# One encoder layer on one core: the first FFN product starts on six tiles' unmixed blocks, and no tile pair is computed plainly

## The chip, the cores and the metric

The kernel runs on one core of a Trainium2 chip. TensorE (PE in the profile) multiplies matrices, VectorE (DVE), ScalarE (ACT) and GpSimd (POOL) work on tiles in SBUF, and DMA queues, issued here by SyncE (SP), move tiles between HBM and SBUF. The metric is the device time of one execution in microseconds (us); lower is better.

## The reference

The layer is a hybrid attention block and then a gated feed-forward network (FFN), over 1024 tokens of 1024 channels, in float32. Only the second part is touched by the change:

```
h2 = rms_norm(x, g_norm2) * (1.0 + sc2) + sh2     # 1024 x 1024
a, up = split(h2 @ w_ffn_in, 2)                   # 1024 x 2816 each
x = x + gt2 * ((silu(a) * up) @ w_ffn_out)
```

The first product, `h2 @ w_ffn_in`, is called FFN1 below.

## The kernel before

**Three passes.** Every float32 operand of a large product is split in two parts, `hi` and `lo`, both in fp32r, and each 128 x 128 x 512 step is three matmuls (hi·hi, hi·lo, lo·hi: `PASS`). A weight block is loaded with `wload` (256 KB, a `raw` tile, 6 buffers) and split with `wsplit`: ACT copies it to `hi` (L101), POOL or, where the caller names it, DVE subtracts to get `lo` (L102). There are 10 `hi` and 10 `lo` buffers, used in turn; a split therefore can't be written before PE has read the split that stood ten places earlier.

**FFN1 in tiles.** The 2816 channels of `a` and `up` are 22 tiles of 128; tile `j` and tile `j + 11` (`HT` is 11) go together in the second FFN product. For one tile the product is a 2 x 2 block product: rows are a and up, the inner blocks are the two halves of the 1024 channels, the columns are the two halves of the tokens. `blk(k, c)` is channel half `k` of token half `c` in `h2T`. A plain tile needs 8 block products of 4 k-steps times 3 passes, 96 matmuls. A tile in the seven-product (Winograd) form needs 7, 84 matmuls: four of them use the mixed token blocks `t1` to `t4`, sums and differences of the four `blk`, and three use unmixed blocks (`w11` with `blk(0,0)`, `w12` with `blk(1,0)`, `x4` with `blk(1,1)`). The weights `x1` to `x4` are sums and differences too, made by `pair_weights` on DVE (L1068, L1069) and POOL (L1076, L1080). `make_t` builds the mixed blocks row by row: for each of 4 rows, 4 additions of hi and lo (L1040, half on POOL), 4 differences (L1042 to L1045), 4 ACT copies (L1048) and 4 subtractions (L1049).

**The order.** PE's order is the program's. The other engines' orders are laid out by a planner at build time, by readiness and then by program order. Ahead of FFN1 stands the output projection in three sweeps of token rows; after each sweep `o_post` finishes the residual and the norm of its token tiles (last step on POOL, L936), and `o_turn` transposes them on PE (L945) into `h2T` (L949, L950). Tokens 0 to 767 are in `h2T` when FFN1 begins; those of tiles 6 and 7 are still in `o_post`. So FFN1 runs tiles 0 and 11 plainly: first their token half 0, 96 matmuls, then `o_turn(6)` and `o_turn(7)`, then `pair_weights` of tile 1 and `make_t` (in program order), then the other token half, 96 matmuls, and from there the pairs (1, 12), (2, 13) and so on by `ffn1_pair`. Tile 1 (`first`) has its three unmixed products first.

**After the products.** `silu_up` applies the sigmoid (ACT, L994), multiplies (DVE L995, POOL L996) and stores; when the second tile of a pair is done it also makes four combinations for the second FFN product (L1003 to L1006). These tiles, the outputs `c11` to `c22`, and the temporaries of `make_t` share one tag `c` with `NC` = 11 buffers. `bank` gives PSUM banks: 4 tags (t, v, d, s) with 2 buffers each.

Of the kernel before, what the change touches and what calls it, by code (L numbers as in the profile page):

```python
# [10 lines left out]
F32 = mybir.dt.float32  # L11
F32R = mybir.dt.float32r
AF = mybir.ActivationFunctionType
# [7 lines left out]
HT = 11  # L21
EPS = 1e-6
NEG = -1e30
NRAW, NHL = 6, 10
NC = 11
W2C = ((), (0,), (1, 2), (3,), (4, 5), (6, 7), (8, 9), (10,))
PP, QT, AQ, AT, AV = 100, 0, 0, 0, 0
WARM = 40
# [7 lines left out]
def hybrid_layer(ctx: ExitStack, tc: tile.TileContext, x, colp, wada1, wada2, bada2, wqkv, wg, wpa, wpb,  # L36
                 wo, w1, w2, hgain, ropeg, rope, rbias, bmask, g2r, out):
    nc = tc.nc

    def pool(name, side, **kw):  # L40
        return tc.alloc_tile_pool(name=name, bufs=1, side=side, reuse_waits="tile", **kw)

    const = pool("const", "left")
    wp = pool("w", "left")
# [13 lines left out]
    def bank(tag):  # L58
        return ps.tile([128, 512], F32, tag=tag, name="ps_" + tag)
# [32 lines left out]
    def wload(src, n):  # L92
        raw = wp.tile([128, 512], F32, tag="raw", bufs=NRAW, name="raw")
        nc.sync.dma_start(raw[:, :n], src)
        return raw[:, :n]

    def wsplit(r, eng=None):
        n = r.shape[1]
        hi = wp.tile([128, 512], F32R, tag="hi", bufs=NHL, name="whi")
        lo = wp.tile([128, 512], F32R, tag="lo", bufs=NHL, name="wlo")  # L100
        nc.scalar.activation(hi[:, :n], r, AF.Copy)  # L101
        (eng or nc.gpsimd).tensor_sub(lo[:, :n], r, fview(hi[:, :n]))  # L102
        return hi, lo

    def wslot(src, n):
        return wsplit(wload(src, n))
# [13 lines left out]
    PASS = ((0, 0), (0, 1), (1, 0))  # L120
# [448 lines left out]
    def mm_set(pb, wsl, src, ksrc, n, ntot, done, hs):  # L569
        for j in range(n):  # L570
            for i, (a, b) in enumerate(PASS):
                nc.tensor.matmul(pb, wsl[a][:, j * 128:(j + 1) * 128], src[b][:, ksrc + j, hs],  # L572
                                 start=(done == 0 and j == 0 and i == 0),
                                 stop=(done + j == ntot - 1 and i == 2))
# [161 lines left out]
    for n in range(6, 92):  # L736
        u, t = divmod(n, 8)
# [70 lines left out]
    mgp = pool("merged", "right")  # L808
# [97 lines left out]
    h2T = [h2p.tile([128, KT, S], F32R, name=f"h2T{i}") for i in range(2)]  # L906
# [77 lines left out]
            for t in ts:  # L984
                o_post(t, [pb[t, 0], pb[t, 1]])

    glate = []
    wj = {}

    gt = {}  # L990
# [1 line left out]
    def silu_up(j, hf, a, up):  # L992
        sg = gt[j, hf] = half_tile("c", NC)
        nc.scalar.activation(sg, a, AF.Sigmoid)  # L994
        nc.vector.tensor_mul(sg, sg, a)  # L995
        nc.gpsimd.tensor_mul(sg, sg, up) if j not in (0, HT) else nc.vector.tensor_mul(sg, sg, up)  # L996
        r, k = divmod(j, HT)
        n = {(0, 0): 0, (1, 0): 1, (1, 1): 2}.get((r, hf))
        if n is not None:
            nc.sync.dma_start(ga_d[n, k], sg)  # L1000
        if r == 1 and hf == 1:
            a11, a21, a12, a22 = (gt[z] for z in ((k, 0), (k, 1), (j, 0), (j, 1)))
            nc.gpsimd.tensor_add(a22, a21, a22)  # L1003
            nc.gpsimd.tensor_sub(a21, a11, a21)
            nc.gpsimd.tensor_sub(a11, a22, a11)
            nc.vector.tensor_sub(a12, a12, a11)  # L1006
            for n, z in enumerate((a22, a11, a21, a12)):
                nc.sync.dma_start(ga_d[3 + n, k], z)

    def ffn1(j, hf):  # L1010
        if j not in wj:
            wj[j] = [wslot(w1[j, :, 4 * q:4 * q + 4, :], 512) for q in range(4)]
        w = wj[j]
        hs = slice(hf * 512, hf * 512 + 512)
        tg = {(0, 0): "vv", (HT, 1): "tt"}.get((j, hf), "ds")
        pa, pu = bank(tg[0]), bank(tg[1])
        for q in range(2):
            mm_set(pa, w[q], h2T, 4 * q, 4, 8, 4 * q, hs)
        for q in range(2):
            mm_set(pu, w[2 + q], h2T, 4 * q, 4, 8, 4 * q, hs)  # L1020

        def post():
            silu_up(j, hf, pa, pu)

        glate.append(post) if glate is not None else post()

    def blk(k, c):
        return [z[:, 4 * k:4 * k + 4, 512 * c:512 * c + 512] for z in h2T]

    def half_tile(tag, bufs):  # L1030
        return sp.tile([128, 512], F32, tag=tag, bufs=bufs, name=tag)

    def make_t():
        tb = [[sp.tile([128, 4, 512], F32R, name=f"t{n}{i}") for i in range(2)] for n in range(4)]
        b = {(k, c): blk(k, c) for k in range(2) for c in range(2)}
        for k in range(4):
            y = {}
            for n, kc in enumerate(((0, 1), (0, 0), (1, 1), (1, 0))):
                y[kc] = half_tile("c", NC)
                (nc.gpsimd if n % 2 else nc.vector).tensor_add(y[kc], fview(b[kc][0][:, k]), fview(b[kc][1][:, k]))  # L1040
            y11, y12, y21, y22 = y[0, 0], y[0, 1], y[1, 0], y[1, 1]
            nc.vector.tensor_sub(y11, y12, y11)  # L1042
            nc.vector.tensor_sub(y12, y22, y12)
            nc.vector.tensor_sub(y22, y22, y11)
            nc.gpsimd.tensor_sub(y21, y21, y22)  # L1045
            for n, z in enumerate((y11, y22, y12, y21)):
                hi, lo = tb[n][0][:, k], tb[n][1][:, k]
                nc.scalar.activation(hi, z, AF.Copy)  # L1048
                (nc.gpsimd if n == 3 else nc.vector).tensor_sub(lo, z, fview(hi))  # L1049
        return tb  # L1050

    nprod = [0]

    def prod(w, b):
        nprod[0] += 1
        pb = bank("tvds"[nprod[0] % 4])
        for k in range(4):
            for i, (p, q) in enumerate(PASS):
                nc.tensor.matmul(pb, w[p][:, k * 128:(k + 1) * 128], b[q][:, k],  # L1059
                                 start=(k == 0 and i == 0), stop=(k == 3 and i == 2))  # L1060
        return pb

    def pair_weights(j, part):
        if part == 0:
            r = wj[j] = {q: wload(w1[j, :, 4 * q:4 * q + 4, :], 512) for q in (0, 2, 3, 1)}
            r["w11"] = wsplit(r[0])
            s1, s2 = (wp.tile([128, 512], F32, tag="raw", bufs=NRAW, name="ws") for _ in range(2))
            nc.vector.tensor_add(s1, r[2], r[3])  # L1068
            nc.vector.tensor_sub(s2, s1, r[0])  # L1069
            r["x2"] = wsplit(s2, nc.vector)  # L1070
            r["w12"] = wsplit(r[1])
            r["s1"], r["s2"] = s1, s2
            return
        r = wj[j]
        s3, s4 = r[2], r["s2"]
        nc.gpsimd.tensor_sub(s3, r[0], s3)  # L1076
        r["x3"] = wsplit(s3, nc.vector)
        r["x1"] = wsplit(r["s1"])
        r["w22"] = wsplit(r[3])
        nc.gpsimd.tensor_sub(s4, r[1], s4)  # L1080
        r["x4"] = wsplit(s4, nc.vector)

    def ffn1_pair(j, first=False):
        for part in range(2):
            if not first:
                pair_weights(j, part)
        w11, x2, w12, x3, x1, w22, x4 = (wj[j][z] for z in ("w11", "x2", "w12", "x3", "x1", "w22", "x4"))
        t1, t2, t3, t4 = tb
        p1 = prod(w11, blk(0, 0))
        c11 = half_tile("c", NC)  # L1090
        nc.scalar.activation(c11, p1, AF.Copy)
        if first:
            p2 = prod(w12, blk(1, 0))
            p3 = prod(x4, blk(1, 1))
        p6 = prod(x2, t2)
        c12 = half_tile("c", NC)
        nc.vector.tensor_add(c12, c11, p6)
        if not first:
            p2 = prod(w12, blk(1, 0))
        nc.vector.tensor_add(c11, c11, p2)  # L1100
        p7 = prod(x3, t3)
        c21 = half_tile("c", NC)
        c22 = half_tile("c", NC)
        nc.vector.tensor_add(c21, c12, p7)
        p5 = prod(x1, t1)
        nc.vector.tensor_add(c22, c21, p5)
        nc.vector.tensor_add(c12, c12, p5)
        p4 = prod(w22, t4)
        nc.vector.tensor_add(c21, c21, p4)  # L1109
        silu_up(j, 0, c11, c21)  # L1110
        if not first:
            p3 = prod(x4, blk(1, 1))
        nc.vector.tensor_add(c12, c12, p3)
        silu_up(j, 1, c12, c22)

    first = 1
    for j, hf in ((0, 0), (HT, 0), (0, 1), (HT, 1)):
        ffn1(j, hf)
        if (j, hf) == (HT, 0):
            o_turn(6)  # L1120
            o_turn(7)
            wop.release()
            mgp.release()
            sp = pool("st", "right")
            for f in glate:
                f()
            glate = None
            pair_weights(first, 0)
            pair_weights(first, 1)
            tb = make_t()  # L1130
    for k in range(1, HT):
        ffn1_pair(k, k == 1)
        ffn1_pair(k + HT)
    sp.release()
    h2p.release()

# [182 lines left out]
```

## Time and profile before

| | |
|---|---|
| Median of 3 runs | 1606.36 us (1603.22 to 1607.03) |
| The profiled execution: its own time | 1605.34 us |
| Its span, first to last instruction | 1603.6 us |
| PE busy | 1542.5 us of the span |
| DVE, ACT, POOL busy | 1026.6, 667.1, 717.3 us |

The span is what the views of the trace cover; 1.7 us lie around it. Time 0 of a view is the start of the span. A line such as L1059 is a line of the kernel before; L1059 is the matmul of `prod`, L572 that of the plain tiles (`mm_set`). Busy time of a matmul includes the time in which it overlaps the next one.

### The profile page before, as it was taken

The page shows a single profiled execution, that of the slowest core. Times are in us where ns is not written, and L with a number is a line of the kernel's source. Part 1 is how long each engine was busy: PE and PEld are TensorE (multiplying, and loading weights), DVE is VectorE, ACT ScalarE, POOL GpSimd, SP SyncE. Part 2 cuts the span into 40 slices and gives each one's busy share as a digit, 9 for nine tenths or more (in the row PEclk, how much of TensorE's full clock was granted, in tenths as well). Part 3 has the DMA queues.
Part 4 walks back from the last instruction along what each step waited for, and adds up shares of the span by engine and source line. Part 5 has one row for each costly group of instructions (what it writes and reads, how often), then busy time and mean ns, then how long its engine had stood idle before and what let it go on. Part 6 is the DMA issues. An engine that isn't in the chain of part 4 may idle for free.

```text
span 1603.6 us, 24772 instructions
## 1 busy us (share of the span) xinstructions
PE 1542.5 (96%) x8240; PEld 1289.0 (80%) x8240; DVE 1026.6 (64%) x2188; ACT 667.1 (42%) x1734; POOL 717.3 (45%) x672
## 2 busy tenths in 40 slices
PE   8999999999999999999999886999999999999997
PEld 7888888898888777778887675788888888888886
DVE  6766676766988743342438869866666666435466
ACT  5555555555645443412234533323333333344442
POOL 1432232221101041554425576876666666545566
PEclk9999999999999999999999998999999999999999
DMA  9322231344244351776645531333333333576765
GB/s 342 101 99 80 84 114 46 125 126 128 88 129 134 92 170 61 264 233 208 210 161 175 177 93 40 104 114 105 101 107 101 106 99 119 191 217 197 243 217 177
DMA packets 149056, 227.52 MB, mean 142 GB/s; under 512 B 27312, under 2 KB 65072, under 8 KB 148928
## 3 DMA queue, kind: packets, MB, share of 16 engines
q1 hardware_dynamic: 148928, 225.94, 44.1%
q8 instruction: 65, 1.06, 0.3%
q14 instruction: 63, 0.52, 0.1%
HBM read 172.28 MB, written 53.59 MB: 141 GB/s over the span
## 4 chain that ended last, share of the span: by engine, by line
PE 75%; DVE 12%; DMA 6%; issue 3%; ACT 2%; POOL 2%; SPq 0%; POOLq 0%; DVEq 0%; ACTq 0%
PE ps_d L283 14%; PE ps_t L1059 6%; PE ps_s L1059 6%; PE ps_v L1059 6%; PE ps_d L1059 6%; PE ps_d L594 4%; PE ps_s L572 3%; PE ps_d L572 3%; PE ps_s L1161 3%; PE ps_d L1161 3%; PE ps_v L475 2%; PE ps_s L434 2%; PE ps_v L1161 2%; PE ps_t L1161 2%; PE ps_t L572 2%
## 5 line engine op out<-in xcount | busy, mean ns | idle before, releaser
L102 POOL TENSOR_TENSOR wlo<-raw,whi 128x512 fp32r<-128x512 f32 (+2 forms) x269 | 362.2, 1354 | 466.6 <-ACT whi L101 442.7
L101 ACT ACTIVATE whi<-raw 128x512 fp32r<-128x512 f32 (+2 forms) x418 | 244.1, 604 | 435.3 <-DMA raw<-in_wg_dram 70.9
L283 PE MATMUL ps_d<-whi,hT 128*128 128x384 f32 x1152 | 316.9, 343 | 0.5 <-ACT v L318 0.5
L102 DVE TENSOR_TENSOR wlo<-raw,whi 128x512 fp32r<-128x512 f32 (+1 forms) x149 | 150.9, 1022 | 130.3 <-ACT whi L101 119.9
L283 PEld LDWEIGHTS ps_d<-whi,hT 128*128 128x128 f32 x1152 | 210.3, 188 | 6.2 <-ACT vs L321 3.5
L283 PE MATMUL ps_d<-wlo,hT 128*128 128x384 f32 x576 | 193.7, 336 | 0.9 <-POOL wlo L102 0.9
L283 PEld LDWEIGHTS ps_d<-wlo,hT 128*128 128x128 f32 x576 | 108.5, 188 | 1.5 <-POOL wlo L102 1.5
L313 POOL TENSOR_TENSOR ra<-qn,rtab 128x64 f32<-128x64 f32 x48 | 16.7, 348 | 166.1 <-DVE qn L306 122.3
L996 POOL TENSOR_TENSOR c<-c 128x512 f32<-128x512 f32 x40 | 63.7, 1593 | 50.2 <-DVE c L1109 42.6
L101 ACT ACTIVATE whi<-ws 128x512 fp32r<-128x512 f32 x60 | 37.9, 632 | 115.0 <-DVE ws L1069 30.0
L449 ACT ACTIVATE P<-P,st 128x256 f32<-128x256 f32 (+2 forms) x100 | 46.2, 464 | 69.5 <-DVE st L448 69.4
L1059 PE MATMUL ps_t<-t,whi 128*128 128x512 f32 x160 | 52.3, 408 | 13.3 <-DVE c L995 12.2
L304 DVE TENSOR_REDUCE ss<-sq 128x4 f32<-128x256 f32 x80 | 33.2, 415 | 45.9 <-ACT sq L301 45.8
L449 ACT ACTIVATE P<-P,sx 128x384 f32<-128x384 f32 (+1 forms) x64 | 37.1, 580 | 52.8 <-DVE sx L448 52.8
L475 PE MATMUL ps_v<-PT,v 128*64 128x128 f32 (+1 forms) x672 | 55.0, 284 | 1.6 <-DVE PT L464 1.6
L460 PE MATMUL ps_t<-ident,P 128*128 128x128 f32 (+1 forms) x336 | 51.6, 274 | 4.5 <-DVE P L452 1.9
L995 DVE TENSOR_TENSOR c<-c 128x512 f32<-128x512 f32 x40 | 46.5, 1162 | 14.2 <-ACT c L994 14.2
L594 PE MATMUL ps_d<-hT,whi 128*128 128x512 f32 x176 | 55.4, 396 | 0.0
L434 PE MATMUL ps_s<-qk 64*128 64x256 f32 (+3 forms) x492 | 53.7, 321 | 1.8 <-DVE st L448 1.2
L572 PE MATMUL ps_s<-hT,whi 128*128 128x512 f32 x176 | 54.3, 390 | 0.0
L434 PEld LDWEIGHTS ps_s<-qk 64*128 64x128 f32 (+1 forms) x492 | 34.9, 182 | 23.6 <-issue 12.5
L448 DVE CUSTOM_DVE_ANT_0 P<-ps_s,rb 128x384 f32<-128x384 f32 (+1 forms) x64 | 31.3, 517 | 33.7 <-PE ps_s L434 33.7
(360 smaller groups left out, 4015.8 us busy)
## 6 DMA issues: line engine op xcount, KB each, us to landing
raw<-in_w_dram SPq DMA_DIRECT2D x165, 256.0 KB
ga_d<-c SPq DMA_DIRECT2D x77, 256.0 KB
raw<-ga_d SPq DMA_DIRECT2D x77, 256.0 KB
wa<-in_wada_dram SPq DMA_DIRECT2D x32, 512.0 KB
raw<-in_wqkv_dram SPq DMA_DIRECT2D x80, 192.0 KB
raw<-in_wo_dram SPq DMA_DIRECT2D x48, 256.0 KB
w_d<-raw SPq DMA_DIRECT2D x44, 256.0 KB
raw<-w_d SPq DMA_DIRECT2D x44, 256.0 KB
```

Source lines behind the costliest of these rows:

```text
L101: nc.scalar.activation(hi[:, :n], r, AF.Copy)
L102: (eng or nc.gpsimd).tensor_sub(lo[:, :n], r, fview(hi[:, :n]))
L283: nc.tensor.matmul(pd[:, :384], tok(a, k, t), U.w[k][b][:, :384], start=(k == 0 and i == 0), stop=(k == KT - 1 and i == 2))
L434: nc.tensor.matmul(I.pS[h][:nq, :nk], U.qk[a][hs, I.q0:I.q0 + nq], U.qk[2 + b][hs, I.kb0 * 128:I.kb0 * 128 + nk], start=(i == 0), stop=(i ...
L449: nc.scalar.activation(P[:nq, :nk], P[:nq, :nk], AF.Exp, scale=-1.0, bias=nm, accum_out=sm)
L460: nc.tensor.transpose(pt[:, i * 128:i * 128 + nq], P[:nq, i * 128:(i + 1) * 128], ident[:nq, :nq])
L475: nc.tensor.matmul(po[hs, :nq], U.v[:, I.kb0 + i, hs], I.PT[h][:, i, :nq], start=(i == 0), stop=(i == nkb - 1))
L572: nc.tensor.matmul(pb, wsl[a][:, j * 128:(j + 1) * 128], src[b][:, ksrc + j, hs], start=(done == 0 and j == 0 and i == 0), stop=(done + j ...
L594: nc.tensor.matmul(st["p"], gw[i, br][j][a][:, kk * 128:(kk + 1) * 128], hT[b][:, k, hs], start=(k == 0 and q == 0), stop=(k == 7 and q == 2))
L996: nc.gpsimd.tensor_mul(sg, sg, up) if j not in (0, HT) else nc.vector.tensor_mul(sg, sg, up)
L1059: nc.tensor.matmul(pb, w[p][:, k * 128:(k + 1) * 128], b[q][:, k], start=(k == 0 and i == 0), stop=(k == 3 and i == 2))
L1161: nc.tensor.matmul(pb[m], o[0][a][:, m * 128:(m + 1) * 128], o[1][b], start=(k == 0 and i == 0), stop=(k == HT - 1 and i == 2))
```

## The change

Tiles 0 and 11 are no longer plain: all 22 tiles take the seven-product form. Six tiles (`EARLY`: 0, 11, 1, 12, 2, 13) run their first two products (`w11`, `w12`, both with token half 0) ahead of everything that needs the mixed blocks: two tiles before `o_turn(6)`, four after it. Their sums are kept in a new tag `e` with 12 buffers; `c` has 8. The four mixed products of tiles 0 and 11 run together, row by row: row k of all eight products, then row k + 1. Tiles 1, 12, 2 and 13 then need five products each. Weight combinations come from `late_weights`, which loads the four blocks of a tile again for the six early tiles. `t1` takes no buffer of its own: it is written over `blk(0,1)` in `h2T`. The diff, without the removed functions (they stand above):

```diff
-NC = 11
+NC, NE = 8, 12
+EARLY = (0, HT, 1, HT + 1, 2, HT + 2)
...
-        nc.gpsimd.tensor_mul(sg, sg, up) if j not in (0, HT) else nc.vector.tensor_mul(sg, sg, up)
+        nc.gpsimd.tensor_mul(sg, sg, up)
...
-        tb = [[sp.tile([128, 4, 512], F32R, name=f"t{n}{i}") for i in range(2)] for n in range(4)]
+        tb = [blk(0, 1)] + [[sp.tile([128, 4, 512], F32R, name=f"t{n}{i}") for i in range(2)] for n in range(1, 4)]
...
+    def prod_bank(tag=None):
+        nprod[0] += 1
+        return bank(tag or "tvds"[nprod[0] % 4])
+
+    def prod_k(pb, w, b, k):
+        for i, (p, q) in enumerate(PASS):
+            nc.tensor.matmul(pb, w[p][:, k * 128:(k + 1) * 128], b[q][:, k],
+                             start=(k == 0 and i == 0), stop=(k == 3 and i == 2))
...
+    def first_weights(j):
+        for q, nm in ((0, "w11"), (1, "w12")):
+            wj[j, nm] = wslot(w1[j, :, 4 * q:4 * q + 4, :], 512)
+
+    def late_weights(j):
+        r = {q: wload(w1[j, :, 4 * q:4 * q + 4, :], 512) for q in (0, 2, 3, 1)}
+        s1, s2 = (wp.tile([128, 512], F32, tag="raw", bufs=NRAW, name="ws") for _ in range(2))
+        nc.vector.tensor_add(s1, r[2], r[3])
+        nc.vector.tensor_sub(s2, s1, r[0])
+        if (j, "w11") not in wj:
+            wj[j, "w11"] = wsplit(r[0])
+        wj[j, "x2"] = wsplit(s2, nc.vector)
+        if (j, "w12") not in wj:
+            wj[j, "w12"] = wsplit(r[1])
+        s3, s4 = r[2], s2
         nc.gpsimd.tensor_sub(s3, r[0], s3)
+        wj[j, "x3"] = wsplit(s3, nc.vector)
+        wj[j, "x1"] = wsplit(s1)
+        wj[j, "w22"] = wsplit(r[3])
         nc.gpsimd.tensor_sub(s4, r[1], s4)
+        wj[j, "x4"] = wsplit(s4, nc.vector)
+
+    def first_prods(j, tags=(None, None)):
+        wj[j, "p"] = prod(wj[j, "w11"], blk(0, 0), tags[0]), prod(wj[j, "w12"], blk(1, 0), tags[1])
+
+    def first_out(j):
+        p1, p2 = wj[j, "p"]
+        c11, c12 = cs[j] = [half_tile("e", NE) for _ in range(2)]
+        nc.scalar.activation(c12, p1, AF.Copy)
+        nc.vector.tensor_add(c11, c12, p2)
+
+    MIX = ("x2", 1), ("x3", 2), ("x1", 0), ("w22", 3)
+
+    def mixed_together(js):
+        pbs = {j: [prod_bank() for _ in MIX] for j in js}
+        for k in range(4):
+            for j in js:
+                for pb, (nm, n) in zip(pbs[j], MIX):
+                    prod_k(pb, wj[j, nm], tb[n], k)
+        for j in js:
+            pair_out(j, iter(pbs[j]))
...
+    def ffn1_pair(j):
+        late_weights(j)
+        if j not in cs:
+            first_prods(j)
+            first_out(j)
+        pair_out(j)
+
+    for j in EARLY[:4]:
+        first_weights(j)
+    first_prods(EARLY[0], "vv")
+    first_prods(EARLY[1], "ds")
+    o_turn(6)
+    o_turn(7)
...
+    for n, j in enumerate(EARLY):
+        if n > 1:
+            if n > 3:
+                first_weights(j)
+            first_prods(j)
+        first_out(j)
+    tb = make_t()
+    for j in EARLY[:2]:
+        late_weights(j)
+    mixed_together(EARLY[:2])
+    for j in EARLY[2:] + tuple(i for k in range(len(EARLY) // 2, HT) for i in (k, k + HT)):
+        ffn1_pair(j)
```

`pair_out` holds the rest of the former `ffn1_pair`: the additions of the mixed products to the sums, `silu_up` for both token halves, and the product `x4` with `blk(1,1)`.

More of the change, by code (lines that the diff above doesn't have):

```diff
@@ L985, in hybrid_layer @@
                 o_post(t, [pb[t, 0], pb[t, 1]])
-    glate = []
     wj = {}
@@ L1008, in silu_up @@
                 nc.sync.dma_start(ga_d[3 + n, k], z)
[L1010 to L1025, printed above, removed]
     def blk(k, c):
@@ L1052, in hybrid_layer, with prod @@
     nprod = [0]
-    def prod(w, b):
+    def prod_bank(tag=None):
         nprod[0] += 1
-        pb = bank("tvds"[nprod[0] % 4])
+        return bank(tag or "tvds"[nprod[0] % 4])
[3 more added lines that the diff above has]
+                             start=(k == 0 and i == 0), stop=(k == 3 and i == 2))
+    def prod(w, b, tag=None):
+        pb = prod_bank(tag)
         for k in range(4):
-            for i, (p, q) in enumerate(PASS):
-                nc.tensor.matmul(pb, w[p][:, k * 128:(k + 1) * 128], b[q][:, k],
-                                 start=(k == 0 and i == 0), stop=(k == 3 and i == 2))
-        return pb
@@ L1063, in pair_weights @@
[L1063 to L1075, printed above, removed]
+            prod_k(pb, w, b, k)
@@ L1076, in pair_weights @@
         nc.gpsimd.tensor_sub(s3, r[0], s3)
-        r["x3"] = wsplit(s3, nc.vector)
-        r["x1"] = wsplit(r["s1"])
-        r["w22"] = wsplit(r[3])
+        wj[j, "x3"] = wsplit(s3, nc.vector)
+        wj[j, "x1"] = wsplit(s1)
+        wj[j, "w22"] = wsplit(r[3])
         nc.gpsimd.tensor_sub(s4, r[1], s4)
[L1081 to L1101, printed above, removed]
+        wj[j, "x4"] = wsplit(s4, nc.vector)
@@ new lines, in hybrid_layer @@
+    cs = {}
+    def first_prods(j, tags=(None, None)):
[14 more added lines that the diff above has]
+            pair_out(j, iter(pbs[j]))
@@ L1102, in ffn1_pair, with pair_out @@
+    def pair_out(j, ps_=None):
+        c11, c12 = cs[j]
+        p = ps_ or (prod(wj[j, nm], tb[n]) for nm, n in MIX)
+        nc.vector.tensor_add(c12, c12, next(p))
         c21 = half_tile("c", NC)
         c22 = half_tile("c", NC)
-        nc.vector.tensor_add(c21, c12, p7)
-        p5 = prod(x1, t1)
+        nc.vector.tensor_add(c21, c12, next(p))
+        p5 = next(p)
         nc.vector.tensor_add(c22, c21, p5)
         nc.vector.tensor_add(c12, c12, p5)
-        p4 = prod(w22, t4)
-        nc.vector.tensor_add(c21, c21, p4)
+        nc.vector.tensor_add(c21, c21, next(p))
@@ L1110, in ffn1_pair @@
         silu_up(j, 0, c11, c21)
-        if not first:
-            p3 = prod(x4, blk(1, 1))
+        p3 = prod(wj[j, "x4"], blk(1, 1))
         nc.vector.tensor_add(c12, c12, p3)
         silu_up(j, 1, c12, c22)
[L1116 to L1130, printed above, removed]
@@ L1131, in hybrid_layer @@
-    for k in range(1, HT):
-        ffn1_pair(k, k == 1)
-        ffn1_pair(k + HT)
+    def ffn1_pair(j):
[10 more added lines that the diff above has]
+    o_turn(7)
+    wop.release()
+    mgp.release()
+    sp = pool("st", "right")
+    for n, j in enumerate(EARLY):
[4 more added lines that the diff above has]
+        first_out(j)
```

## The prediction

> **What bounds the kernel now.** I read the page first, then the stretches around FFN1, then single instructions there.
>
> ```profile
> span 1603.6 us, 24772 instructions
> PE 1542.5 (96%) x8240; PEld 1289.0 (80%) x8240; DVE 1026.6 (64%) x2188; ACT 667.1 (42%) x1734; POOL 717.3 (45%) x672
> ```
>
> PE is busy for 96% of the span, so a change pays in two ways only: fewer matmuls, or fewer holes between them. The table of stretches shows where the holes of FFN1 are (columns: length, then busy time and instruction count of each engine, then the granted PE clock).
>
> ```profile
> core 0: us, PE busy (x) PEld busy (x) DVE busy (x) ACT busy (x) POOL busy (x), PEclk, DMA share, GB/s
> 932.95:958.25 25.30, 24.09 (x115) 19.69 (x113) 16.55 (x26) 6.95 (x19) 18.52 (x11) 1.00 0.26 73
> 958.25:988.80 30.55, 30.32 (x132) 24.70 (x132) 29.99 (x30) 11.79 (x19) 18.54 (x12) 1.00 0.15 44
> 988.80:1007.46 18.66, 5.35 (x14) 3.63 (x13) 18.03 (x19) 8.61 (x16) 12.54 (x8) 0.63 0.16 52
> 1007.46:1046.30 38.84, 38.84 (x169) 31.54 (x168) 30.04 (x31) 11.99 (x20) 31.61 (x22) 1.00 0.34 104
> 1046.30:1385.00 338.70, 338.70 (x1466) 275.28 (x1465) 221.57 (x253) 105.25 (x174) 227.21 (x163) 1.00 0.34 106
> ```
>
> From 1007.46 on PE never stops. From 988.80 to 1007.46 it does 5.35 us of work, while DVE is busy for 18.03 of 18.66 us: DVE is building the mixed blocks. PE's own timeline shows the edges.
>
> ```profile
> 932.95 0.70 PE L572 MATMUL ps_v<-h2T,whi 128*128 128x512 f32 x2
> ...
> 954.84 1.04 PE L945 MATMUL ps_t<-ident,tm 128*128 128x128 f32 x8
> 956.94 1.16 PE L945 MATMUL ps_t<-ident,tm 128*128 128x128 f32 x8 [1.06 <-DVE h2T L950]
> 958.25 0.50 PE L572 MATMUL ps_d<-h2T,whi 128*128 128x512 f32 x1 [0.15 <-ACT h2T L949]
> ...
> 988.55 0.39 PE L1059 MATMUL ps_s<-h2T,wlo 128*128 128x512 f32 x1
> 1001.10 1.22 PE L1059 MATMUL ps_t<-t,whi 128*128 128x512 f32 x2 [12.16 <-DVE c L995]
> ...
> 1006.88 0.51 PE L1059 MATMUL ps_t<-t,whi 128*128 128x512 f32 x1 [1.15 <-DVE t L1049]
> ```
>
> The 12.16 us are put down to a bank that DVE had not emptied (L995). But behind it stands the mixed block itself: the last row of `t2` came at 1006.88. Freeing the bank alone would have brought little.
>
> The price of products, from the chain of waits:
>
> ```profile
> 933.19 10.91 PE ps_v L572 x48
> 1010.42 2.81 PE ps_d L1059 x12
> 1016.04 2.74 PE ps_t L1059 x12
> ```
>
> A plain matmul is 10.91 / 48 = 0.227 us. A product of 12 that reads a `t` tile (1010.42) takes 2.81, one that reads `h2T` (1016.04) 2.74. The second hole is 18.66 - 2.81 = 15.85 us of loss. The first, around `o_turn`: from 932.95 to 958.25 there are 96 matmuls (21.8) and 16 transposes (2 x 1.04), so 25.3 - 23.9 = 1.4 us are lost.
>
> **Part 1: fewer matmuls.** Two plain tiles cost 192 x 0.227 = 43.6 us. In the new form a tile has three products on `t` tiles (8.43) and four on `h2T` (10.96), since `t1` now lies there: 19.39, for two 38.8. Saved: 4.8 us. The other 20 tiles read `t1` from `h2T` too, 20 x 0.07 = 1.4 us. Together 6.2 us, if the price goes with the place of the tile. The Trainium skill (SBUF — State Buffer, "SBUF: two separate sides") says PE's port never waits for another engine; by that the place would be worth nothing and the gain 4.8 us. The two rows above differ by 0.07 us all the same, so I follow them.
>
> **Part 2: `o_turn` comes earlier.** Only 48 matmuls stand ahead of it, not 96: PE wants it at 932.95 + 10.91 = 943.9. What it waits for is the end of the norm, on DVE and POOL:
>
> ```profile
> 940.71 0.69 DVE L1068 TENSOR_TENSOR ws<-raw 128x512 f32<-128x512 f32 x1
> 941.49 1.82 DVE L1069 TENSOR_TENSOR ws<-ws,raw 128x512 f32<-128x512 f32 x1
> 943.30 2.47 DVE L935 SCALAR_TENSOR_TENSOR tm<-xt,ry,sc 128x1024 f32<-128x1024 f32 x2
> 944.72 6.11 POOL L936 TENSOR_TENSOR tm<-tm,sh 128x1024 f32<-128x1024 f32 x2 [1.96 <-DVE tm L935]
> 926.24 1.94 PE L945 MATMUL ps_t<-ident,tm 128*128 128x128 f32 x8 [5.68 <-DVE h2T L950]
> ```
>
> POOL's two additions end at 947.8 and 950.8. The two weight sums of tile 1 (940.71, 941.49) sit inside that chain; in the new program the sums come four loads later, so up to 2 us of it can go. On the other hand four more early splits of POOL may take that place. I take 947 for tile 6, and the end of `o_turn(7)` at 950.5 (949.5 to 952). Loss: 950.5 - 943.9 - 2.1 = 4.5 us instead of 1.4. After the 5.68 us wait of row 926.24 eight transposes took 1.94 instead of 1.04 us: a long wait halves PE's speed for some us. The wait here is 3 us in two pieces; I add 0.5 (0 to 2). If `first_out` of tile 0 is held up as well, the bank of the next product adds some 1.5 us; ACT is idle there (6.95 of 25.3 us), so I count nothing. The 96 early products then end at 950.5 + 0.5 + 21.8 = 972.8.
>
> **Part 3: the mixed blocks against the row-by-row products.** What DVE and POOL need for `make_t` sets the pace:
>
> ```profile
> 972.50 0.68 DVE L1049 TENSOR_TENSOR t<-c,t 128x512 fp32r<-128x512 f32 x1
> 978.20 1.77 DVE L1049 TENSOR_TENSOR t<-c,t 128x512 fp32r<-128x512 f32 x1
> 979.90 1.77 DVE L1040 TENSOR_TENSOR c<-h2T,h2T 128x512 f32<-128x512 f32 x1
> 977.70 1.73 POOL L1045 TENSOR_TENSOR c<-c 128x512 f32<-128x512 f32 x1
> 979.39 1.74 POOL L1040 TENSOR_TENSOR c<-h2T,h2T 128x512 f32<-128x512 f32 x1
> 1003.97 2.86 DVE L1049 TENSOR_TENSOR t<-c,t 128x512 fp32r<-128x512 f32 x2
> 1010.89 1.74 POOL L1049 TENSOR_TENSOR t<-c,t 128x512 fp32r<-128x512 f32 x1
> ```
>
> A DVE instruction takes 0.68 us alone (0.60 from start to start) and 1.77 when a POOL instruction of 1.7 us runs: the two take turns, one of each per 1.70 us. From 958.25 to 1007.46 there were 49 DVE and 20 POOL instructions: 20 x 1.70 + 29 x 0.60 = 51.4 against 49.2 measured. So I can price a changed list.
>
> The list after `o_turn(7)`. DVE: 2 for `h2T`, 32 of `make_t`, 4 sums of `first_out`, 2 splits left of tile 0, 4 instructions for tile 11: 44. The eight `silu` instructions and the start of tile 12 that stood there before are gone. POOL: 12 of `make_t` (4 of its 16 can run before, as now), 3 for tile 0, 3 for tile 11: 18. That is 18 x 1.70 + 26 x 0.60 = 46.2 us, so 996.7 if nothing idles. The other bound is the present pace: POOL's last split of a row ended at 1010.89 + 1.74 = 1012.6, 54.4 us after `o_turn`, which gives 950.5 + 54.4 = 1004.9. I take 1001, the middle, because the list is shorter but its last rows still wait for ACT and POOL in turn.
>
> PE needs 22.5 us for the 96 mixed matmuls (8 x 2.81) and would be through at 995.3; it waits for the last row. After that come at least 15 matmuls (`w22` of tile 0, four products of tile 11), 3.5 us, at half speed 6.5: I take 5. So the mixed pairs end at **M** = 1006 (1000 to 1012).
>
> **The sum.** Before, 136 products remained at 1007.46 and took 377.5 us (79 on `t`, 57 on `h2T`). After M there remain 134, 60 on `t` and 74 on `h2T`: 19 x 2.81 less, 17 x 2.74 more, 6.8 us less. M comes 1.5 us earlier. The next four tiles need 14 us each instead of 19.4, with little less work beside them; I add 1.5 us (0 to 4) of waits there. Change: -1.5 - 6.8 + 1.5 = -6.8 us. The profiled execution took 1605.34, so 1598.5; the median of the runs is 1.0 higher: about 1599.5, which I round to 1600. The 3 MB of weights loaded twice cost nothing: DMA is at 0.15 to 0.26 of its time here. If that cover failed, one block of 256 KB at the 104 GB/s of the next stretch would be 2.5 us late. On SP's queue these loads stand ahead of the stores of `silu`, for which nothing waits here. The four products of `silu` that go from DVE to POOL fall behind M, and are in its 1.5 us. The `c` buffers (8 for `make_t`'s temporaries) allow two rows in flight, as the old 11 less the waiting `silu` tiles did.
>
> A measurement tells apart about 0.3%, 4.8 us, so "faster" is below 1601.6.
>
> **The rivals.**
>
> Weights of tile 11 come last (slower). `late_weights` of tile 11 is last in program order, and its buffers come free only as tile 0's splits are done. PE's order wants all eight weights in row 0. If `w22` of tile 11 is ready at 1000, after the whole list, 75 matmuls remain: 17.5 + 2 for the slow clock gives M = 1019.5, and 13.5 us more than above: 1613. It decides once that split is later than 986.5. For it: the planner's program order. Against it: before, the first weight sum of tile 12 ran as early as DVE had it loaded, inside `make_t`. Chance 0.2.
>
> PE's clock stays down between rows. Four rows took 49 us, 12 us each, and a row costs PE 5.6 us, so PE waits some 6 us before each. The row at 1001.10, after 12.16 us, needs 1.22 us for two matmuls, where 0.70 is normal (row 932.95); a last row of 24 at nearly twice the price lasts some 10 us instead of the 5 that I took, M = 1011, 1605. Here the Trainium skill (TensorE: Matmul & The Clock Gate, "Why this matters for your kernels") speaks against the change: no holes over about 3 us. Chance 0.1.
>
> The list runs without idling and its cover is full: M = 1000, no later waits: 7.5 us better, 1592. Against it: today's tail on POOL. Chance 0.12.
>
> The four short tiles are bound by DVE and POOL. In the long stretch (338.7 us, 17.4 tiles) DVE is busy 12.7 and POOL 13.0 us per tile. A short tile drops two POOL splits, but if every DVE instruction on SBUF met a POOL one, DVE needs 7.5 x 1.70 + 6 x 0.67 = 16.8 us against 14.0: four tiles lose 11 us, 1609. Against it: with the mean prices of that stretch it is 12 us. Chance 0.08.
>
> **How the numbers follow.** The forecast has chance 0.5, its own range 1593 to 1607; that part gives faster 0.3, same 0.17, slower 0.03. The full-cover case adds 0.12 to faster. The clock case gives 0.08 same and 0.02 faster, the short tiles 0.04 same and 0.04 slower, tile 11's weights 0.06 same and 0.14 slower. Sums: faster 0.44, same 0.35, slower 0.21. The range goes from the full-cover case to the weights case, 1592 to 1613; the half of the latter above it and the tail below it are left out.
>
> **What would show it.** Right: a hole of 3 to 5 us at `o_turn(6)`; then 96 matmuls without a hole; row waits on L1049 or its successors in the mixed products, which end near 1006; 12-matmul products on `t1` at 2.74; no hole after. Wrong: a wait on a `whi` or `wlo` of tile 11 in the first row (weights case); holes on weights in tiles 1 to 13 (short tiles); or PE waiting for a PSUM bank after `o_turn(7)`, which I priced at nothing.

## The result, and the profile after

The changed kernel is slower: 1609.95 us median (20 runs) against 1604.99 us for the kernel before in the same comparison, a ratio of 1.0028 with a 95% interval of 1.0017 to 1.0039. I had forecast 1600, 6 us under the kernel before. It became 5 us more: inside the stated range of 1592 to 1613, but on the other side of the kernel before.

The page of the changed kernel:

```profile
span 1608.7 us, 24829 instructions
PE 1547.8 (96%) x8216; PEld 1293.0 (80%) x8216; DVE 1044.9 (65%) x2208; ACT 662.7 (41%) x1742; POOL 744.6 (46%) x680
```

There are 24 matmuls fewer, as intended, and the span is 5.1 us longer. FFN1 now starts at 932.31 (before 932.95) and ends at 1390.14 (before 1385.00): 457.83 us instead of 452.05. From its end to the end of the span it is 218.6 us in both. So the whole difference lies inside FFN1. Its stretches, with the columns of the table in the prediction:

```profile
core 0: us, PE busy (x) PEld busy (x) DVE busy (x) ACT busy (x) POOL busy (x), PEclk, DMA share, GB/s
932.31:955.20 22.89, 14.76 (x67) 11.72 (x65) 18.72 (x28) 10.23 (x25) 20.43 (x12) 0.82 0.43 130
955.20:979.68 24.48, 24.48 (x97) 20.05 (x97) 22.63 (x25) 8.56 (x15) 20.49 (x12) 0.89 0.11 33
979.68:1001.14 21.46, 9.50 (x24) 5.67 (x23) 21.46 (x21) 7.63 (x14) 16.04 (x10) 0.62 0.18 50
1001.14:1019.91 18.77, 18.77 (x74) 15.10 (x73) 6.57 (x11) 4.77 (x8) 6.31 (x5) 0.89 0.06 18
1019.91:1390.14 370.23, 370.23 (x1610) 302.45 (x1608) 268.63 (x297) 108.92 (x195) 274.00 (x186) 1.00 0.36 114
```

The first row is the 48 early matmuls and `o_turn`: 8 us without work. The second is the other 96 early products. The third is the first row of the mixed products: PE works 9.50 of 21.46 us and DVE does not pause. In the fourth the other rows run through without a hole. From 1019.91, where the mixed products are done (M in the prediction), PE never stops again. PE's timeline names what ended each hole (L1083 is the DVE sum of `first_out`, L1082 its ACT copy, L103 the lo half of a split):

```profile
946.71 1.63 PE L946 MATMUL ps_t<-ident,tm 128*128 128x128 f32 x8 [3.21 <-POOL tm L937]
951.93 1.94 PE L946 MATMUL ps_t<-ident,tm 128*128 128x128 f32 x8 [3.59 <-DVE h2T L951]
955.20 1.22 PE L1043 MATMUL ps_v<-h2T,whi 128*128 128x512 f32 x2 [1.32 <-ACT e L1082]
...
987.52 1.22 PE L1043 MATMUL ps_t<-t,whi 128*128 128x512 f32 x2 [5.58 <-DVE e L1083]
...
993.28 0.79 PE L1043 MATMUL ps_v<-t,wlo 128*128 128x512 f32 x1 [3.27 <-DVE wlo L103]
...
1000.12 1.22 PE L1043 MATMUL ps_t<-t,whi 128*128 128x512 f32 x2 [3.09 <-DVE e L1083]
```

The three lower holes stand in the first row of the mixed products, in front of `w22` of tile 0, the third matmul of `x2` of tile 11 (the one that needs the lo half of the split) and `w22` of tile 11. The first and the last are waits for a PSUM bank of an early tile (12, then 13) that DVE has not added up yet. The middle one is a late weight split; the expectations of a2 and a4 below call it the split of `x3`, but it reads `ws`, from which `x2` is made (DVE 991.48, done at 993.2). None is a wait for a mixed block. DVE's and POOL's timelines show these instructions and the work around `o_turn`:

```profile
948.38 2.81 DVE L1060 TENSOR_TENSOR ws<-ws,raw 128x512 f32<-128x512 f32 x1 [1.17 <-POOL wlo L103]
951.11 1.28 DVE L951 TENSOR_TENSOR h2T<-ps_t,h2T 128x512 fp32r<-128x512 f32 x2
...
986.79 0.68 DVE L1083 TENSOR_TENSOR e<-e,ps_t 128x512 f32<-128x512 f32 x1
...
991.48 1.75 DVE L103 TENSOR_TENSOR wlo<-ws,whi 128x512 fp32r<-128x512 f32 x1
...
999.39 0.67 DVE L1083 TENSOR_TENSOR e<-e,ps_t 128x512 f32<-128x512 f32 x1
```

```profile
943.34 3.32 POOL L937 TENSOR_TENSOR tm<-tm,sh 128x1024 f32<-128x1024 f32 x1
946.62 1.72 POOL L103 TENSOR_TENSOR wlo<-raw,whi 128x512 fp32r<-128x512 f32 x1
948.30 2.34 POOL L937 TENSOR_TENSOR tm<-tm,sh 128x1024 f32<-128x1024 f32 x1
...
966.13 5.22 POOL L1028 TENSOR_TENSOR c<-c 128x512 f32<-128x512 f32 x1 [3.70 <-DVE c L1027]
...
1004.18 1.27 POOL L1032 TENSOR_TENSOR t<-c,t 128x512 fp32r<-128x512 f32 x1
```

At `o_turn` a weight split (946.62) stands between POOL's two additions, and a weight sum (948.38, 2.81 us) stands on DVE ahead of the copy that frees `o_turn`'s bank. The last mixed block was complete at 1004.18 + 1.27 = 1005.5; PE was then still 14 us from M.

### The profile page after: what moved, and what is told of

Same layout as the page of the kernel before. It is cut to its first block, busy times and chain, and to the rows that moved or that the text cites. A ratio compares the mean times of both kernels' runs of the same rounds, so it can differ in the third digit from the quotient of the medians.

```text
span 1608.7 us, 24829 instructions
## 1 busy us (share of the span) xinstructions
PE 1547.8 (96%) x8216; PEld 1293.0 (80%) x8216; DVE 1044.9 (65%) x2208; ACT 662.7 (41%) x1742; POOL 744.6 (46%) x680
## 4 chain that ended last, share of the span: by engine, by line
PE 73%; DVE 11%; DMA 6%; issue 4%; POOL 3%; ACT 2%; SPq 0%; POOLq 0%; DVEq 0%; ACTq 0%
PE ps_d L284 15%; PE ps_v L1043 6%; PE ps_d L1043 6%; PE ps_t L1043 6%; PE ps_s L1043 6%; PE ps_d L595 4%; PE ps_s L1168 3%; PE ps_d L1168 3%; PE ps_s L573 3%; PE ps_d L573 3%; PE ps_v L476 2%; PE ps_s L435 2%; PE ps_v L1168 2%; PE ps_t L1168 2%; PE ps_t L461 2%
## 5 line engine op out<-in xcount | busy, mean ns | idle before, releaser
L103 POOL TENSOR_TENSOR wlo<-raw,whi 128x512 fp32r<-128x512 f32 (+2 forms) x267 | 366.4, 1380 | 431.5 <-ACT whi L102 407.9
L103 DVE TENSOR_TENSOR wlo<-raw,whi 128x512 fp32r<-128x512 f32 (+1 forms) x151 | 154.6, 1032 | 128.0 <-ACT whi L102 119.6
L102 ACT ACTIVATE whi<-ws 128x512 fp32r<-128x512 f32 x66 | 41.3, 626 | 184.0 <-DVE ws L1060 142.1
L996 POOL TENSOR_TENSOR c<-c 128x512 f32<-128x512 f32 x44 | 72.4, 1645 | 56.9 <-DVE c L1107 47.2
L1059 DVE TENSOR_TENSOR ws<-raw 128x512 f32<-128x512 f32 x22 | 26.3, 1194 | 71.7 <-POOL wlo L103 61.5
L305 DVE TENSOR_REDUCE ss<-sq 128x4 f32<-128x256 f32 x80 | 33.3, 416 | 47.5 <-ACT sq L302 47.4
L1043 PE MATMUL ps_v<-h2T,whi 128*128 128x512 f32 x184 | 58.8, 402 | 1.3 <-ACT e L1082 1.3
L1043 PE MATMUL ps_s<-h2T,whi 128*128 128x512 f32 x184 | 57.7, 395 | 0.0
L995 DVE TENSOR_TENSOR c<-c,e 128x512 f32<-128x512 f32 x44 | 49.4, 1123 | 12.3 <-ACT c L994 12.3
L1043 PE MATMUL ps_d<-h2T,whi 128*128 128x512 f32 x176 | 54.5, 391 | 0.0
```

## The experiments

The start of FFN1 moves between 929.7 and 936.4 us from profile to profile, in stages that no edit touches. So beside the totals I compare two lengths of each profile: FFN1 from its first matmul to the first of the second FFN product, and the time from the same start to M. Each length is of one profile; the changed kernel and a3, whose engines turn out to work in the same order, differ by 0.12 us in it.

| kernel | FFN1 us | start to M | ratio to before (95%) |
|---|---|---|---|
| before | 452.05 | (74.5 to the same count of matmuls) | 1 |
| changed | 457.83 | 87.6 | 1.0028 (1.0017 to 1.0039) |
| a1 product by product | 460.77 | 90.6 | 1.0078 (1.0060 to 1.0095) |
| a2 tile 11 later | 454.76 | 84.5 | 1.0024 (1.0013 to 1.0036) |
| a3 weights first | 457.95 | 87.7 | 1.0040 (1.0027 to 1.0053) |
| a4 ACT empties | 457.88 | 87.6 | 1.0035 (1.0022 to 1.0047) |
| b three ahead | 457.75 | 87.5 | 1.0029 (1.0016 to 1.0042) |
| b four early | 460.57 | 79.4 | 1.0053 (1.0040 to 1.0067) |
| c1 ready order | 450.99 | 80.7 | 0.9994 (0.9984 to 1.0005) |
| c2 ready order, three ahead | 447.44 | 77.1 | 0.9986 (0.9973 to 0.9999) |
| d1 named banks | 455.15 | 77.3 | 1.0016 (1.0002 to 1.0030) |
| d2 second ready order | 448.48 | 78.2 | 0.9987 (0.9972 to 1.0002) |
| e1 lo parts by ACT | 445.31 | 75.1 | 0.9956 (0.9940 to 0.9973) |
| e2 banks of x4 too | 449.04 | 77.6 | 0.9974 (0.9958 to 0.9989) |

For a1 and b three ahead, "start to M" is worked out: in a1 from the end of tile 0's four products plus four more of 2.8 us, in three ahead from the end of FFN1 less 370.2 us; for four early less 370.2 and 11 us, since 48 early matmuls are made later there.

**a1: is the row order used?** The call of `mixed_together` is replaced:

```diff
-    mixed_together(EARLY[:2])
+    for j in EARLY[:2]:
+        pair_out(j)
```

> The mixed products of tiles 0 and 11 run one after the other, not row by row; all else as in the changed kernel, where the mixed products ended at 1019.9 us of the span (call this M). If the rows of the mixed blocks decide (the step of the prediction), the first product has to wait for the last row of t2, ready near 1001, and 96 matmuls of 22.5 us follow: M near 1023 to 1026, total 4 to 6 us longer than the changed kernel. If banks and weights of the first row decide in the changed kernel, product by product needs one bank and one weight at a time, all waits but that for t2 vanish, and M is near 1023 too, but the holes on a bank (L1083) and on a split (L103) are gone. So the time says what row by row is worth: at most 3 to 6 us instead of the 15 or so that its full use would give.

In the mixed products PE waited for rows of `t2`, and no longer for a bank or a split:

```profile
993.67 0.80 PE L1043 MATMUL ps_v<-t,whi 128*128 128x512 f32 x1 [10.14 <-ACT t L1031]
1001.11 0.80 PE L1043 MATMUL ps_v<-t,whi 128*128 128x512 f32 x1 [6.64 <-DVE t L1032]
...
1004.00 0.80 PE L1043 MATMUL ps_v<-t,whi 128*128 128x512 f32 x1 [0.83 <-DVE t L1032]
```

Row by row is worth 3 us (90.6 to 87.6), a fifth of the 15 that I had thought possible. The total rose by more than that, since this program's FFN1 also began 4 us later; why the stages ahead of it took longer there, I did not settle.

**a2: the first row of tile 11 later.**

```diff
-        for k in range(4):
-            for j in js:
+        for j, k in ((0, 0), (0, 1), (1, 0), (1, 1), (0, 2), (1, 2), (0, 3), (1, 3)):
+            j = js[j]
...
```

> Order of the mixed steps: rows 0 and 1 of tile 0, rows 0 and 1 of tile 11, then row 2 of both, row 3 of both. Theory that tile 11's banks and splits decide (in the changed kernel its x3 split came at 993.2, its last bank at 1000.1): 12 matmuls of tile 0 fill part of the hole, 63 instead of 75 remain after 1000, M falls by about 3 us from 1019.9 to 1016 or 1017. Theory that the mixed rows decide: the last row was complete at 1005.5, so M would stay where it is or follow the row, and the gain is 0.

DVE's order is the same as in the changed kernel, instruction by instruction, so only PE's order differs. The wait for the split is gone, the bank is still as late:

```profile
987.68 1.22 PE L1043 MATMUL ps_t<-t,whi 128*128 128x512 f32 x2 [6.12 <-DVE e L1083]
...
1000.34 0.94 PE L1043 MATMUL ps_t<-t,whi 128*128 128x512 f32 x2 [3.98 <-DVE e L1083]
```

M came 3.1 us earlier, as expected of the theory that tile 11's first row decides. Other work was ready behind it.

**a3: weights ahead of `make_t` in the program.** `for j in EARLY[:2]: late_weights(j)` stands before `tb = make_t()`.

> late_weights of tiles 0 and 11 stand ahead of make_t in program order. If the splits of tile 11 hold the first row (weights theory), the hole on L103 vanishes and M falls by up to 3 us plus what follows from it; the DVE and POOL instructions of make_t shift by up to 10 and 8 places, so its last row comes later than 1005.5. If the sums of first_out, which free the banks, decide (banks theory), M stays at 1019 to 1021, with the holes on L1083 as before.

Nothing moved: the matmuls after the three holes start within 0.1 us of the changed kernel's (987.60, 993.37 and 1000.21 against 987.52, 993.28 and 1000.12). The planner put the instructions in the same places, so this run says nothing on weights against banks; it says that the place in the program does not set their order here.

**a4: ACT empties the banks.**

```diff
-        nc.vector.tensor_add(c11, c12, p2)                  # first_out
+        nc.scalar.activation(c11, p2, AF.Copy)
...
+        nc.vector.tensor_add(c11, c11, c12)                 # pair_out
```

> first_out empties both banks of a tile by ACT copies; the DVE sum of the two is made after the mixed products, on SBUF. Banks theory: the holes of 5.58 and 3.09 us in front of w22 go, the hole on the x3 split of tile 11 (993.2) and its w22 split (997.7) remain; M = 997.7 + 75 x 0.2335 + about 1 = 1016 to 1017, 3 us less. If the mixed rows decide, M stays. If ACT's copies stand as late in ACT's order as DVE's sums stood in DVE's, the holes stay, with ACT as the one waited for.

M did not move. The holes changed owner:

```profile
987.13 1.22 PE L1043 MATMUL ps_v<-t,whi 128*128 128x512 f32 x2 [8.93 <-ACT whi L102]
...
991.63 0.79 PE L1043 MATMUL ps_v<-t,wlo 128*128 128x512 f32 x1 [3.27 <-DVE wlo L103]
...
997.26 1.22 PE L1043 MATMUL ps_t<-t,whi 128*128 128x512 f32 x2 [2.28 <-ACT e L1083]
```

Without the DVE sums, the split of `x2` of tile 11 is what PE waits for first, and the last bank, now emptied by ACT, comes as late as before: 67.6 us after the start of FFN1, against 67.8. Banks and splits are two waits, one close behind the other, and easing one leaves the other.

**b: four early tiles, and three tiles ahead of `o_turn`.** The first is `EARLY = (0, HT, 1, HT + 1)`; the second moves one tile:

```diff
     first_prods(EARLY[1], "ds")
+    first_prods(EARLY[2], "ds")
     o_turn(6)
...
-        if n > 1:
+        if n > 2:
```

> Only four tiles early (0, 11, 1, 12): 48 matmuls of 10.9 us go from before the mixed products to after them. The eight banks of the mixed products are then free early (the last early sums stand for tiles 1 and 12). If the banks decide, M falls by 3 to 6 us, and the time rises by 5 to 8. If DVE, POOL and the splits decide, M stays and the time rises by 11. If M falls by 11, PE's own work decided and the time stays.

> Three tiles (72 matmuls, not 48) stand ahead of o_turn(6). PE wants it at 932.3 + 16.4 = 948.7, when POOL has nearly finished it, so the hole at o_turn shrinks from 9.7 us to 3 to 5 and the slow clock after it goes. If that hole was part of the loss, the time falls by 5 to 8 us. If it only moved a wait that stands further on (DVE and POOL finish the banks and splits of tile 11 at the same time whatever PE does), M stays within 2 us of 1020 and the time with it: the hole cost nothing.

With four early tiles M falls by 8.2 us, between two of the expected cases (3 to 6, and 11), and 11 us of products come later: 2.7 us longer. Here no bank and no split is waited for in the mixed products. The mixed rows decide, the step that I had forecast for the changed kernel, and the last hole is POOL's part of a row:

```profile
994.08 0.51 PE L1043 MATMUL ps_v<-t,whi 128*128 128x512 f32 x1 [1.57 <-DVE t L1032]
...
999.28 0.50 PE L1043 MATMUL ps_t<-t,whi 128*128 128x512 f32 x1 [2.84 <-POOL t L1032]
```

With three tiles ahead FFN1 is as long as in the changed kernel (457.75). The hole in front of `o_turn(6)` is gone, and another came behind it:

```profile
954.97 1.94 PE L946 MATMUL ps_t<-ident,tm 128*128 128x128 f32 x8 [5.54 <-DVE h2T L951]
...
966.50 1.22 PE L1043 MATMUL ps_s<-h2T,whi 128*128 128x512 f32 x2 [9.60 <-DVE e L1083]
```

So the hole at `o_turn(6)` cost the changed kernel nothing: without it, PE waits longer further on.

**c: the mixed steps in the order in which their inputs come.** The 32 steps (product, row, tile) are listed by hand, by the times of the changed kernel's trace: first two rows of `x2`, `x3` and `x1` of tile 0, then tile 11 as its splits arrive, row 3 last. c2 has three tiles ahead of `o_turn` besides.

```diff
-        for k in range(4):
-            for j in js:
-                for pb, (nm, n) in zip(pbs[j], MIX):
-                    prod_k(pb, wj[j, nm], tb[n], k)
+        for jj, q, k in STAIR:
+            j, (nm, n) = js[jj], MIX[q]
+            prod_k(pbs[j][q], wj[j, nm], tb[n], k)
```

> The 32 mixed steps of tiles 0 and 11 (4 products x 4 rows x 2 tiles, 3 matmuls each) stand in the order in which the trace of the changed kernel shows their last input: rows 0 and 1 of tile 0 first, then what needs tile 11's splits (993 to 998), row 2 (998), tile 11's last bank (1000.1), row 3 (996.6 to 1005.5). Theory that the first row of tile 11 (banks and splits) holds back work that is ready: nearly all of it runs in the former holes, six or seven steps remain after 1001 and two after 1005.5; M falls from 1019.9 to 1007 to 1010, total 9 to 12 us less than the changed kernel, under the kernel before. Theory that DVE and POOL as a whole are too slow (the rows decide anyway): the gain is what the tile 11 order gave, about 3 us, and no more.

> Both edits: the ready order of the mixed steps, and three tiles ahead of o_turn. If DVE and POOL set the end of the mixed blocks, it is no faster than the ready order alone (within 2 us). If the hole at o_turn counts once the rows do not hold PE, it is 2 to 5 us faster than the ready order alone.

c1 gains 6.8 us of FFN1, between the two expectations: I had put `x2` of tile 11 too early in the list, and PE stood 5.0 and 3.3 us before it. c2 gains 10.4 us and is the first version whose total lies under the kernel before with its whole interval, by a hair (0.9973 to 0.9999). Now the hole at `o_turn` counts, 3.6 us. PE's stretch to M:

```profile
932.21:1009.35 77.14, 60.97 (x259) 49.31 (x257) 67.63 (x76) 29.23 (x58) 63.84 (x36) 0.89 0.23 68
1009.35:1379.65 370.30, 370.30 (x1609) 302.24 (x1608) 270.35 (x300) 110.16 (x197) 273.25 (x187) 1.00 0.36 114
```

**d: named banks, and a second order.** d1 names the banks of the early tiles so that those that ACT or `o_turn` frees come first; d1 and d2 have three tiles ahead of `o_turn`, as c2, and a second list, with tile 11's `x2` later.

```diff
-            first_prods(j)
+            first_prods(j, ("vd", "dt", "tv")[n - 3])
...
-        pbs = {j: [prod_bank() for _ in MIX] for j in js}
+        pbs = {j: [prod_bank(t) for t in ts] for j, ts in zip(js, ("ssvd", "dttv"))}
```

> Three tiles ahead of o_turn, mixed steps in the order in which the trace of the earlier such version shows their inputs (last input 1005.1), and the banks of tiles 12, 2 and 13 named so that the first ones are those that ACT or o_turn frees, not those that a DVE sum frees. If the 9.02 us hole on a DVE sum at 966.2 held PE back, it vanishes and the mixed products end as soon as their last row allows: M from 1009.3 to 1006 or 1007, FFN1 from 447.4 to 444 to 446 us. If the hole only moved a wait that stands further on, the length of FFN1 stays at 447 to 448.

> As the version with three tiles ahead and ready order, with the second ready order and the old banks. In that version PE waited only 1.6 us in the mixed steps, so the order of the steps can give at most that: FFN1 445.5 to 448 us. It separates the order from the banks in the run beside it.

In d1 c2's hole of 9.02 us in front of an early product is gone and M stays at 77.3: rows decide now, with waits of up to 4.2 us for L1032. FFN1, 455.15 us, fits neither expectation. I had overlooked the next bank, that of `x4`, which now held a product that is emptied late:

```profile
983.38 0.79 PE L1043 MATMUL ps_d<-t,whi 128*128 128x512 f32 x1 [4.19 <-POOL t L1032]
...
1002.43 0.50 PE L1043 MATMUL ps_d<-t,whi 128*128 128x512 f32 x1 [0.68 <-POOL t L1032]
...
1013.57 1.22 PE L1043 MATMUL ps_v<-h2T,whi 128*128 128x512 f32 x2 [5.49 <-DVE e L1107]
```

d2 is as long as c2 within 1.1 us, on the longer side and just above what I expected; the order had nothing left to give.

**t1 alone.** The kernel before with `tb = [blk(0, 1)] + ...`.

> The kernel before with one part of the change alone: t1 is written over blk(0,1) in h2T. Place theory (a product on h2T takes 2.73 to 2.74 us, one on a t tile 2.81): the product with x1 falls to 2.73 in 20 tiles, FFN1 from 452.05 to 450.6 us, nothing to be seen in the total. If a tile's place is worth nothing, x1 stays at 2.81 and FFN1 at 452.0.

The plain products of the second token half then read the overwritten `blk(0,1)`; that part of the computation is changed, and PE has to wait for `make_t` before it, which I had not seen: FFN1 464.87 us. The total is of no use. But the products of the later tiles can be read. One tile's end and the next one's start are, in the chain of waits, `w22` and `x4`, then `w11`, `x2`, `w12`, `x3` and `x1`:

```profile
1103.47 2.81 PE ps_d L1059 x12
1106.28 2.73 PE ps_s L1059 x12
1109.02 2.72 PE ps_t L1059 x12
1111.73 2.81 PE ps_v L1059 x12
1114.54 2.73 PE ps_d L1059 x12
1117.28 2.81 PE ps_s L1059 x12
1120.08 2.73 PE ps_t L1059 x12
```

Three products of a tile take 2.81 us and four 2.72 to 2.73, `x1` (1120.08) among them, where it was four and three: the place of `t1` gives 0.07 to 0.08 us a tile.

**e: work or order?**

```diff
-                (nc.gpsimd if n == 3 else nc.vector).tensor_sub(lo, z, fview(hi))   # make_t
+                nc.scalar.activation(lo, z, AF.Copy)
```

That is e1. e2 is d1 with the products `x4` of tiles 0 and 11 on the `s` banks, and with the turn of the banks begun anew behind them.

> The changed kernel, but the lo parts of the mixed blocks are ACT copies of the block instead of subtractions on DVE (12) and POOL (4): this leaves the subtraction out. If the amount of DVE and POOL work makes banks and splits late, 16 instructions of 0.6 to 1.7 us go from the stretch, the sums of first_out and tile 11's splits come 8 to 15 us earlier, and M falls from 87.6 us after the start of FFN1 to 72 to 80. If only the order of the queues counts (each sum stands behind what it stood behind before, and ACT is now the one with the longer queue), M falls by less than 3 us.

> The version with named banks, with x4 of tiles 0 and 11 on the two banks that are emptied first, so that the 5.49 us hole after the mixed products (and the slow clock behind it) goes. Nothing but the rows of the mixed blocks is left to wait for: the mixed products end 77 us after the start of FFN1, as there, and FFN1 takes 447 to 449 us, 7 to 8 less than with the hole at x4 and no better than the version with three tiles ahead and ready order (447.4). Should it come below 446, the rows did not decide.

In e1, with 16 instructions off DVE and POOL and nothing else changed in the program, M falls by 12.5 us, from 87.6 to 75.1. The waits for a bank and for splits in the first row shrink to 2.7 us and less:

```profile
981.80 0.74 PE L1043 MATMUL ps_t<-t,whi 128*128 128x512 f32 x2 [2.71 <-DVE e L1083]
...
983.55 0.93 PE L1043 MATMUL ps_v<-t,whi 128*128 128x512 f32 x2 [0.77 <-ACT whi L102]
...
989.23 0.51 PE L1043 MATMUL ps_t<-t,wlo 128*128 128x512 f32 x1 [0.73 <-POOL wlo L103]
```

So these 16 instructions in the two queues are enough to make both late. That it is their number alone is not shown: without them the planner also laid the rest of DVE's work in another order, and a row's lo half no longer passes from ACT to DVE or POOL. e2 ends its mixed products at 77.6, as expected, with row waits alone in them; two bank waits are left outside, 1.17 us in front of an early product and 0.53 us in front of `x4`. Its FFN1 is 449.04; in total it is the best of the versions that compute the layer, 0.26% under the kernel before, while d2 and c2 cannot be told from it.

## Why the prediction was wrong

**Fewer matmuls: right.** After M the products took 370.23 us, where the sum said 377.5 - 6.8 = 370.7. The price by place held: `t1` from `h2T` costs 2.73. By the Trainium skill (SBUF — State Buffer, "SBUF: two separate sides") PE never waits for another engine's access, and by that alone the place would be worth nothing. Measured, the two places differ by 3%; the reason is open, since no run here shows whether a wait is behind it.

**The short tiles: right, with less than I had added.** I added 1.5 us of waits for tiles 1, 12, 2 and 13; there were none.

**`o_turn`: mis-sized, but hidden behind later waits in the changed kernel.** I had the end of `o_turn(7)` at 950.5; its last transposes began at 951.93 and took 1.94 us, so it ended at 953.9, outside the 949.5 to 952 that I had allowed. The split and the weight sum that stood in the way are those that I had named, but I took the good case for both. The bank that I counted at nothing cost 1.32 us. After these three holes the clock was 0.89, so the early products ended at 979.68, 47.4 us after the start of FFN1 instead of 39.9. The run with three tiles ahead shows that the hole in front of `o_turn(6)` cost nothing in the changed kernel.

**The step that failed is "it waits for the last row".** I had M at 73 us after the start (1006), by the rows; it was 87.6. In the sum, M's term was -1.5 us and measured +13.1 (87.6 against 74.5); the products gave -7.3 where the sum said -6.8, and the 1.5 us of waits did not come. Two things are in the 14.5 us. The last row came at 1005.5 instead of 1001, 73.1 after the start instead of 68; had it decided, M would have been 5 us later than I said, 4 of them from the later end of `o_turn`. That the rest fitted, 51.6 us from there to the last row against 50.5, was luck in part: 49 DVE and 24 POOL instructions stand in that stretch, not the 44 and 18 of my list, and each cost less than I had priced it. Without waits for banks and splits in the mixed products M stands at 77 to 78 (c2, d1, e2), so the row bound was 4 to 5 us off.

The other 10 us are the first row of tile 11. PE's order asks in row 0 for all eight banks and all eight splits; I checked the splits as a rival and wrote the banks off in one clause. Both came last out of the same full DVE and POOL queues, so that the last item of row 0 was ready at 1000.1 and 75 matmuls stood behind it. Both signs of being wrong that I had named for this stretch came: a wait on a split of tile 11 in the first row, and waits for a bank after `o_turn(7)`. The rival "weights of tile 11 come last", with chance 0.2, has the right M (1019.5 against 1019.9) and the right point of decision, but its number is luck in part: it took `w22` of tile 11 to be split at 1000, the split was done at 997.7 (POOL 996.01, 1.71 us), and it was the bank that came at 1000.1. Its mechanism is half of it: in a2 PE comes later, so the split's wait is gone and the bank's stays, in a4 the DVE sums are gone and the split's stays.

**The clock.** I gave the slow clock between rows a chance of 0.1. It came in the first row, with a granted clock of 0.62 from 979.68 to 1001.14, and went on into the second: from 987.52 to about 1005 two matmuls took 1.05 to 1.22 us where 0.63 is normal. In the rows behind PE had no holes and full speed. That agrees with the Trainium skill (TensorE: Matmul & The Clock Gate, "Why this matters for your kernels"), which asks for no gaps over about 3 us between bursts of matmuls: the holes here were of 5.6, 3.3 and 3.1 us. In the other versions half speed followed holes of 2.7 and 2.8 us too, one to two us behind them (e1, b four early), and the 1.6 us one of c2 was followed by full speed.

**How much of the forecast gain is there.** The forecast amounts to 445.2 us of FFN1. Of the versions that compute the layer, c2 comes nearest, with 447.44. e1 reached 445.31, but with 16 subtractions left out. In the changed kernel the gain was turned into a wait for the first row of tile 11.

## What to carry to other kernels

Running products row by row helps only as far as the first row can start: list for every step in PE's order when each of its inputs comes (block, weight split and PSUM bank), and let PE take them in that order. Where an engine's queue is full, what it delivers late can be late together, as the banks and splits were here, so removing one named wait shows the next one a few us behind; count the work of the queue first. And a hole in front of a later, longer wait costs nothing until the later one is gone.

## What the runs showed of the hardware that I had not expected

DVE and POOL do not always take turns. Where both worked on SBUF, a DVE instruction mostly lasted 1.7 to 1.8 us instead of 0.68. But from 966 to 971 DVE ran eight of its instructions back to back at 0.60 us, and POOL's one subtraction lasted 5.22 us instead of 1.3 to 1.7. So a price of one of each per 1.70 us is too high for such a list: the 49 DVE and 24 POOL instructions from 953.87 to 1005.45 took 51.6 us, where 24 x 1.70 + 25 x 0.60 gives 55.8.
